# A gradient along rows of 8192 x 8192: the loads and stores of one DMA queue in groups of three instead of in strict turn

## The chip, the cores and the metric

The kernel runs on one core of a Trainium2 chip. The time is device microseconds of one execution. All differences here are a few microseconds in 1250, so fast runs are compared with fast runs of the kernel before on the same chip, and where a trace is read, it is one profiled execution. A microsecond in 1250 is 0.08%; most 95% intervals below are about 0.25% wide in all.

## The reference

```python
def reference(x: np.ndarray) -> np.ndarray:      # x: 8192 x 8192 float32
    return np.gradient(x, axis=1)
```

Inside a row the result is half the difference of the two neighbours; in the first and the last column it is the plain difference of two elements. So 268.44 MB are read and 268.44 MB are written, with almost no arithmetic.

## The kernel before

The rows are cut into 32 tiles of 128 partitions x 2 rows (8.389 MB). There are three slots in SBUF. A tile is loaded into a slot, the vector engine writes the halved differences back into the same slot, 64 elements lower, two small instructions put the end columns in place, and the slot is stored. All loads and stores are issued by the sync engine, on one queue.

```python
    def load(i):
        b = slots[i % NB]                                   # NB = 3
        ins = nc.sync.dma_start(out=b[:, SH : SH + W], in_=x_sets[i])
        loads.append(chain(i, ins, *([stores[i - NB]] if i >= NB else [])))

    with tc.manual_schedule():
        for i in range(NB):
            load(i)
        for i in range(nsets):                              # nsets = 32
            ...                                             # GpSimd: end columns; vector engine: the tile
            for r in range(0, R, nr):                       # one pass; two halves for the last tile
                ...
                ins = nc.sync.dma_start(
                    out=out_sets[i, :, r * m : (r + nr) * m], in_=b[:, r * m : (r + nr) * m]
                )
                stores[i] = chain(i, ins, placed)
                if 2 <= i and not last:
                    tc.add_manual_dep(ins.ins, stores[i - 1].ins.name, landed, reason="behind a load that has begun")
                at = [halved]
            if 1 <= i and i - 1 + NB < nsets:
                load(i - 1 + NB)
```

`chain(i, ins, needed...)` makes an instruction wait for the named ones only. The order of the queue is L0 L1 L2 S0 S1 L3 S2 L4 S3 L5 ..., with each store from S2 on (those of the last tile excepted) held back until the store before it has landed.

## Time and profile before

| | kernel before |
|---|---|
| time, median of 3 (and of 6, with the later ones) | 1250.21 us (1250.34) |
| span of the profiled run | 1247.7 us |
| vector engine busy | 554.8 us, 44% |
| DMA queue busy | 99.6% |

The lines that show the bound are in the prediction. The rows behind its last reading, that early turns are slower than late ones, are these: issue rows of the sync engine in the timeline (start, duration, engine, line, operation; the load rows between them are left out). A store is issued there at the moment the previous one has landed, so the steps between rows are the time of one load and one store.

```profile
140.42 0.34 SPq L95 DMA_DIRECT2D out_dram<-slot  x1
...
179.55 0.33 SPq L95 DMA_DIRECT2D out_dram<-slot  x1
...
218.83 0.33 SPq L95 DMA_DIRECT2D out_dram<-slot  x1
...
258.45 0.33 SPq L95 DMA_DIRECT2D out_dram<-slot  x1
...
1072.97 0.33 SPq L95 DMA_DIRECT2D out_dram<-slot  x1
...
1111.62 0.33 SPq L95 DMA_DIRECT2D out_dram<-slot  x1
...
1150.25 0.33 SPq L95 DMA_DIRECT2D out_dram<-slot  x1
```

The late steps are 38.65 and 38.63 us, the early ones half a microsecond to a microsecond longer. The DMA engines are busy in both, and the question of this study is what in the early ones is slow.

### The profile page before, as it was taken

How to read it: one execution, taken by the hardware profiler on the slowest of the kernel's cores; microseconds unless marked ns; L12 is line 12 of the kernel's file. 1: busy time of each engine (PE TensorE's matmuls, PEld its weight loads, DVE VectorE, ACT ScalarE, POOL GpSimd, SP SyncE). 2: the span in 40 equal slices, each digit the busy share in tenths (PEclk: the TensorE clock that was granted, in tenths of full speed). 3: DMA queues.
4: the chain of work that ended last, by engine and by line, in shares of the span. 5: the costliest groups of instructions: out<-in, count | busy, mean ns of one | idle time of the engine just before them, and what ended most of it. 6: DMA issues, size and time to landing. Idle time of an engine off the chain costs nothing.

```text
span 1247.7 us, 241 instructions
## 1 busy us (share of the span) xinstructions
DVE 554.8 (44%) x54; POOL 8.8 (1%) x48
## 2 busy tenths in 40 slices
DVE  2851455324553345533455334554335543355433
POOL 0000000000000000000000000000000000000000
DMA  9999999999999999999999999999999999999998
GB/s 403 437 437 424 424 429 435 435 435 431 431 437 433 427 431 433 429 435 437 437 437 435 427 431 437 427 433 437 437 437 437 435 431 429 435 433 437 431 433 357
DMA packets 9361, 536.88 MB, mean 430 GB/s; under 512 B 1040, under 2 KB 1040, under 8 KB 1040
## 3 DMA queue, kind: packets, MB, share of 16 engines
q1 hardware_dynamic: 9360, 536.88, 99.6%
q14 instruction: 1, 0.01, 0.0%
HBM read 268.44 MB, written 268.44 MB: 430 GB/s over the span
## 4 chain that ended last, share of the span: by engine, by line
another core or an unknown queue 68%; DVE 18%; DMA 8%; issue 3%; POOL 1%; POOLq 0%
DVE slot L82 18%; DMA slot<-in_x_dram 5%; DMA out_dram<-slot 3%; POOL ends L71 0%; POOL slot L93 0%; DVE slot L93 0%; POOLq L129 0%
## 5 line engine op out<-in xcount | busy, mean ns | idle before, releaser
L82 DVE CUSTOM_DVE_ANT_0 slot<-slot 128x16382 f32<-128x16382 f32 (+1 forms) x33 | 551.3, 16706 | 670.6 <-POOL ends L71 670.6
L71 POOL TENSOR_TENSOR ends<-slot 128x4 f32<-128x4 f32 x32 | 6.3, 198 | 991.5 <-DMA slot<-in_x_dram 991.5
L93 DVE COPY slot<-ends 128x4 f32<-128x4 f32 (+1 forms) x21 | 3.6, 171 | 0.7
L93 POOL COPY slot<-ends 128x4 f32<-128x4 f32 x12 | 2.3, 190 | 207.8 <-DVE slot L82 207.8
L118 POOL MEMSET const-bfloat16-1.0<- 128x1 bf16 x1 | 0.1, 102 | 0.0
L118 POOL MEMSET const-uint8-127<- 128x1 uint8 x1 | 0.1, 102 | 0.0
L118 POOL MEMSET const-float32-0.0<- 128x1 f32 x1 | 0.1, 98 | 0.2 <-issue 0.2
L118 POOL MEMSET const-float32-1.0<- 128x1 f32 x1 | 0.1, 98 | 0.0
## 6 DMA issues: line engine op xcount, KB each, us to landing
out_dram<-slot SPq DMA_DIRECT2D x2, 4096.0 KB, 20.2
slot<-in_x_dram SPq DMA_DIRECT2D x32, 57.6
out_dram<-slot SPq DMA_DIRECT2D x31, 38.6
```

The lines of the kernel that those rows point to most:

```text
L71: ins = nc.gpsimd.tensor_sub(out=ends[:, i, :, :], in0=xin[:, :, 1 : m : m - 2], in1=xin[:, :, 0 : m - 1 : m - 2],)
L82: ins = nc.vector._custom_dve(dve_ops.TENSOR_TENSOR_REDUCE_SUB_MAX, out=b[:, c0:c1], in0=b[:, SH + c0 + 1 : SH + c1 + 1], in1=b[:, SH + c0 ...
L93: ins = placer.tensor_copy(out=res[:, :, 0 : m : m - 1], in_=ends[:, i, r : r + nr, :])
L118: nc = _bacc.Bacc("TRN2", target_bir_lowering=False, num_devices=1)
```

## The change

The intent is to let the queue hold runs of three loads and three stores, and to drop the waits that kept loads and stores in strict turn. The instructions, their bytes and the slots stay as they were.

```diff
-    landed = mybir.DependencyInfo(mybir.DependencyClass.Sync, mybir.DependencyReason.DATA)
@@
                 stores[i] = chain(i, ins, placed)
-                if 2 <= i and not last:
-                    tc.add_manual_dep(ins.ins, stores[i - 1].ins.name, landed, reason="behind a load that has begun")
                 at = [halved]
-            if 1 <= i and i - 1 + NB < nsets:
-                load(i - 1 + NB)
+            if i % NB == NB - 1:
+                for k in range(i + 1, min(i + 1 + NB, nsets)):
+                    load(k)
```

The order of the queue becomes L0 L1 L2 S0 S1 S2 L3 L4 L5 S3 S4 S5 ..., and ends L30 L31 S30 and the two halves of S31. The places where a store follows a load fall from 30 to 11, those where a load follows a store from 29 to 10.

> **What bounds the kernel now.** I read the page's shares of busy time first, then the slices, then the issue rows of the sync engine in the timeline, then its waits, then stretches of the span beside each other.
>
> ```profile
> span 1247.7 us, 241 instructions
> DVE 554.8 (44%) x54; POOL 8.8 (1%) x48
> ...
> DMA  9999999999999999999999999999999999999998
> GB/s 403 437 437 424 424 429 435 435 435 431 431 437 433 427 431 433 429 435 437 437 437 435 427 431 437 427 433 437 437 437 437 435 431 429 435 433 437 431 433 357
> ...
> q1 hardware_dynamic: 9360, 536.88, 99.6%
> ```
>
> The vector engine works 44% of the span and GpSimd 1%; the one DMA queue keeps 16 engines busy for 99.6% of it. No slice shows a hole. So the kernel is bound by moving 536.88 MB, and the order of the queue can only matter if it changes the rate or opens holes.
>
> The steady state, in the timeline of one full turn (a column of start, one of duration):
>
> ```profile
> 724.99 0.33 SPq L95 DMA_DIRECT2D out_dram<-slot  x1
> 725.36 0.43 SPq L61 DMA_DIRECT2D slot<-in_x_dram  x1
> 744.29 0.20 POOL L71 TENSOR_TENSOR ends<-slot 128x4 f32<-128x4 f32 x1 [20.92 <-DMA slot<-in_x_dram]
> 744.52 17.22 DVE L82 CUSTOM_DVE_ANT_0 slot<-slot 128x16382 f32<-128x16382 f32 x1 [21.40 <-POOL ends L71]
> 761.78 0.17 DVE L93 COPY slot<-ends 128x4 f32<-128x4 f32 x1
> 763.62 0.33 SPq L95 DMA_DIRECT2D out_dram<-slot  x1
> 764.00 0.43 SPq L61 DMA_DIRECT2D slot<-in_x_dram  x1
> 782.95 0.20 POOL L71 TENSOR_TENSOR ends<-slot 128x4 f32<-128x4 f32 x1 [38.46 <-DMA slot<-in_x_dram]
> ```
>
> Each store is issued at the instant the previous store has landed, and GpSimd starts the instant a load has landed. So a store landed at 724.99, a load at 744.29, a store at 763.62, a load at 782.95: steps of 19.30, 19.33 and 19.33 us, with no difference between the two directions and nothing added at a switch. A tile is 128 partitions x 16384 x 4 bytes = 8.389 MB; 8.389 / 19.32 = 434.2 GB/s. From a load's landing to a finished tile is 761.78 + 0.17 - 744.29 = 17.66 us, less than one transfer.
>
> The waits of the sync engine, total, count, longest:
>
> ```profile
> SPq L95 <- DMA out_dram<-slot: 1082.2, 29, 38.8
> SPq L61 <- DMA out_dram<-slot: 21.5, 1, 21.5
> ```
>
> These 1082.2 us look like a cost and are none: the sequencer waits for the previous store while the load queued behind that store is still to come, which is 19.3 us of work for the DMA engines. The chain of waits on the page puts 68% under "another core or an unknown queue" and 18% under the vector engine; with the DMA slices at 9 throughout, I don't take that attribution as a bound.
>
> Last, the start of the span and later stretches (width, vector busy, GpSimd busy, clock, DMA share, GB/s):
>
> ```profile
> 3.00:60.00 57.00, 34.62 (x3) 0.59 (x3) 1.00 0.99 423
> 105.00:395.00 290.00, 121.25 (x11) 1.98 (x11) 1.00 1.00 432
> 700.00:1185.00 485.00, 223.05 (x20) 3.52 (x18) 1.00 1.00 434
> ```
>
> The DMA is busy in all of them, yet the early rate is a little lower than the late one. The first issue rows show the same: store issues at 140.42, 179.55, 218.83, 258.45 and 297.75 are 39.13, 39.28, 39.62 and 39.30 us apart, where late ones are 38.63. This is all the waste there is. If the first load lands at 22.56 (the issue at 0.74 plus 21.82 in the chain in order of time) and the other 63 transfers took 19.32 us each, the last would land at 22.56 + 63 x 19.32 = 1239.7 us. The span is 1247.7, of which about 1 us is the end after the last landing. So some 7 us, 0.6%, are lost to slow packets, nearly all in the first half.
>
> **What the Trainium skill says.** (1) DMA: Bandwidth & Descriptors, section "Where 436 GB/s comes from": the 16 ports give 435.2 GB/s in all. The trace agrees: 434.2 GB/s in the steady turn is 99.8% of that, for loads and for stores. (2) The same page, section "Anatomy of one DMA": DMA engines don't wait on semaphores, the issuing sequencer does. So an order can only open a hole if the sync engine issues too late; the trace has issues 19 us ahead of need. (3) The same page, section "Queues, rings and completion order": on each engine the descriptors are consumed in ring order. That fits the landings above, which come in the order of issue, and lets me lay out the new order as a simple row of transfers. I found no section that gives a cost for switching between loads and stores; here the trace decides, and it shows none in steady state.
>
> **The change part by part.** Removed: 29 waits of a store for the landing of the previous store. They delayed only the sequencer; worth 0 us by themselves. Added: nothing; the same 32 loads and 33 stores, with the same bytes and same descriptors. The work of the vector engine and GpSimd is the same: 33 x 16.706 us = 551.3 us in all, still hidden if the DMA doesn't wait for it. Moved: the loads of tiles 3k+3 to 3k+5 now stand behind the stores of 3k to 3k+2. Switches of direction fall from about 62 to about 21, worth 0 us each by the steady steps.
>
> Now the new row, with 19.32 us a transfer from the landing of load 2 at about 62 us (GpSimd's start on tile 2 in the trace is at 62.22). Stores 0, 1, 2 are ready at 40.3, 59.7 and 79.9, and are due at 62, 81 and 101: at least 21 us early. Load 3 is issued when store 0 has landed and store 2 was issued, at 81.5; it is due at 120. Load 4 at 101, due at 139; load 5 at 120, when load 3 begins, due at 159. So each load is issued about two transfers (38.6 us) ahead. Load 3 lands at 139, so store 3 is ready at 139 + 17.7 = 157 and due when load 5 ends at 178: 21 us early (2 x 19.32 - 17.66 = 21.0). Store 4 is ready at 158.5 + 17.7 = 176 and due at 197; store 5 at 195.5, due at 217. Load 6 must follow store 5 in program order (195.5) and store 3's landing (197): issued at 197, due at 236. That closes a cycle of 6 x 19.32 = 115.9 us for three tiles, with a smallest slack of 21.0 us, against 115.9 us for three turns of before. No hole opens.
>
> The tail: 32 = 10 x 3 + 2, so the last group has two loads, then store 30, then the two halves of store 31. Store 30 is ready 17.7 us after its load, while load 31 takes 19.32: 1.7 us early. That is the smallest slack of all, and it occurs once. The first half of tile 31 needs 0.2 + 8.7 + 0.2 us, the second as much again, both inside store 30's 19.32. So the row again ends with the same three stores, back to back, as before. Sum: 0 us from waits, 0 from switches, 0 from holes. The 7 us of early slow packets stay to be settled.
>
> **The rivals.**
> Rival A, the early loss belongs to switches: fewer of them would take away up to two thirds of 7 us, giving about 1245.5 us. For it: the early turns of 39.1 to 39.6 us all contain switches. Against it: the late turns contain as many and cost nothing; and three loads in a row, 3 to 60 us, have only 423 GB/s.
> Rival B, the early loss belongs to loads (engines that read in step, or something that passes with time) and comes with grouped loads as well, or a little more because three follow each other: 1250 to 1256 us. For it: the rate of the first three loads, which know no switch; GpSimd's starts on tiles 3 to 6 at 120.92, 160.17, 199.47 and 239.14 with the store issues between show loads of 19.6 to 20.3 us and stores of about 19.4. This is my main case, at the same loss.
> Rival C, the queue runs dry: if a store had to wait for its tile, each group would lose a part of one transfer, 11 x 19.3 = 212 us at most, so some 1460 us. The slack of 21 us per store speaks against it, and the vector engine at 44% too.
> Rival D, the deeper queue: up to four transfers are outstanding now, against three before. A sequencer that blocks on a full ring would delay an issue that has 20 to 38 us of slack. No cost expected.
> Rival E, long runs of stores are slower than single ones. The trace has two in a row, stores 0 and 1, landing at about 81.5 and 101.3 (the load issue and the next store issue at those times): 19.4 and 19.8 us. If each of 32 stores took 0.4 us more, that would be 13 us, 1263 us: still within 2%.
>
> **Range and chances.** The median is 1250.2 us before; my sum moves it by 0, with A pulling to 1245 and B to 1256. I predict 1250 us, 8 in 10 between 1244 and 1257. Faster by over 2% means below 1225, under the 1239.7 that the DMA rate alone allows: chance 0.01. Slower by over 2% means above 1275, and needs C or a slowdown I can't see: 0.03. The rest, 0.96, is within 2%.
>
> **What would show each step right or wrong.** The DMA line should stand at 9 in all slices, the queue's share at 99 to 100%. The sync engine's rows should show three stores about 19 us apart, then loads issued as each store lands, a cycle of 115.9 us late in the span, and its long waits moved from stores waiting for stores to loads waiting for stores and stores for the vector engine or GpSimd. Vector busy time should stay near 555 us. Late steps other than 19.32 us within a run of loads or stores would refute the claim that switches are free; a hole in the DMA slices once per group would make C right; an early loss clearly under 7 us would make A right, one over it B in its stronger form. I would be wrong by more than the range if a run of three loads or stores had another rate than a single one.

## The result, and the profile after

The changed kernel took 1247.49 us (median of 6 runs, 1246.68 to 1248.03) against 1250.34 us before (6 runs, 1249.39 to 1251.82). A ratio here is the mean time of one kernel's fast runs over that of the other's of the same rounds, so it is not quite the ratio of these medians: 0.9976, with a 95% interval of 0.9963 to 0.9989. The change is worth some 3 us or a quarter of a per cent, by the verdict at 2% "same", and the interval leaves out 1.

The page of the changed kernel, busy times, DMA slices and queue:

```profile
span 1245.0 us, 241 instructions
DVE 554.8 (45%) x54; POOL 8.8 (1%) x48
...
DMA  9999999999999999999999999999999999999999
...
q1 hardware_dynamic: 9360, 536.88, 99.8%
```

Compute is unchanged, and the DMA is busy throughout, as before. The sync engine's own waits (for whom, us in total, times, longest):

```profile
SPq L94 <- DVE slot L92: 525.7, 21, 55.9
SPq L60 <- DMA out_dram<-slot: 373.2, 29, 19.2
SPq L94 <- POOL slot L92: 298.8, 12, 36.7
```

The 1082.2 us of stores waiting for stores are gone, and 1197.7 us of other waits stand in their place. None of them is time that the kernel loses: the sequencer has nothing to do in either version. This is how to read a wait on a sequencer that only issues transfers: its length says little, only whether it ended in time does. The issue rows of the changed kernel show that:

```profile
157.57 38.99 SPq L94 DMA_DIRECT2D out_dram<-slot  x3
197.84 39.18 SPq L60 DMA_DIRECT2D slot<-in_x_dram  x3
273.61 39.05 SPq L94 DMA_DIRECT2D out_dram<-slot  x3
313.93 39.12 SPq L60 DMA_DIRECT2D slot<-in_x_dram  x3
...
1203.88 19.93 SPq L94 DMA_DIRECT2D out_dram<-slot  x3
1205.53 0.20 POOL L70 TENSOR_TENSOR ends<-slot 128x4 f32<-128x4 f32 x1 [19.14 <-DMA slot<-in_x_dram]
```

A row with "x3" is three issues, and its duration runs from the first to the last. Store 3 is issued at 157.57 and is due when load 5 lands, at about 178.5; load 6 at 197.84, two transfers before it is due. The smallest margin is at the end: store 30 is issued at 1203.88 and load 31 has landed on all engines at 1205.5 (the last line).

So where do the 2.7 us of the span come from? For that I used two records of the trace that have no view: the time at which each of the 16 DMA engines finished its share of each transfer, and the duration of each 64 KB packet (2.418 us when nothing disturbs it). "Landing" below is the last of the 16, "spread" the last less the first. "Loss" is what the last landing is later than the first landing plus 63 transfers of 19.32 us.

| trace | first landing | last landing | loss, us | spread at the end of the loads, us | packets more than 0.1 us slow | their excess, us over all engines | of it where a store follows a load |
|---|---|---|---|---|---|---|---|
| before | 22.56 | 1246.82 | 7.1 | 5.6 | 160 | 58.8 | 56.2 |
| after | 22.63 | 1244.12 | 4.3 | 2.6 | 95 | 38.8 | 37.0 |

(Packets of the first 6 us are left out, since every kernel has the same slow ones there.) In both kernels some 95% of the excess is of packets under way while a load with a store behind it was landing (from half a microsecond before its first engine finished to half a microsecond after its last). Those stretches are 13% of the span in the kernel before and 2% in the changed one. In the trace before, the spread grows from 0.6 us to 5.4 us in the first 630 us, and after that the steps are 19.32 us with hardly a slow packet; in the changed kernel it grows to 2.6 us. So the picture is: at such a place some engines lose part of a microsecond, those that lose fall behind, and once the engines are far enough apart the losses stop. (The packet records don't name their engine, so that it is the same engines that lose and fall behind is inferred.) How long the loads with a store behind them took in the changed kernel, from landing to landing (the third load of each of the first nine groups; 19.35 us is the undisturbed figure):

```text
load 2: 20.41 us   load 5: 19.36   load 8: 19.36   load 11: 19.39
load 14: 19.85     load 17: 19.95  load 20: 20.01  load 23: 19.52  load 26: 19.62
```

### The profile page after: what moved, and what is told of

It is laid out like the page before. It is cut to its first block, busy times and chain, and to the rows that moved or that the text cites. A ratio compares the mean times of both kernels' runs of the same rounds, so it can differ in the third digit from the quotient of the medians.

```text
span 1245.0 us, 241 instructions
## 1 busy us (share of the span) xinstructions
DVE 554.8 (45%) x54; POOL 8.8 (1%) x48
## 4 chain that ended last, share of the span: by engine, by line
another core or an unknown queue 74%; DVE 18%; DMA 3%; issue 2%; POOL 1%; SPq 0%; POOLq 0%
DVE slot L81 18%; DMA slot<-in_x_dram 3%; POOL ends L70 0%; POOL slot L92 0%; SPq L60 0%; DVE slot L92 0%; POOLq L127 0%
```

## The experiments

Theory S (switch): time is lost where a store follows a load, so fewer such places lose less. Rival L (load): each load loses a little, whatever follows it. Rival W (wait): the removed waits, or the deeper queue without them, are the gain. The results of all runs in one table; "places" are those where a store follows a load.

| kernel | places | time, us | before of the same call, us | ratio (95%) | loss in its trace, us | spread, us |
|---|---|---|---|---|---|---|
| e1_no_wait: strict turn without the waits | 30 | 1250.13 | 1250.64 | 0.9996 (0.9984 to 1.0009) | 6.3 | 5.2 |
| e2_pairs: groups of two | 16 | 1249.32 | 1250.64 | 0.9992 (0.9980 to 1.0005) | 6.2 | 5.2 |
| e4_after_again: the change | 11 | 1247.57 | 1250.64 | 0.9977 (0.9964 to 0.9989) | 4.9 | 2.7 |
| e9_far_stores: the change, other addresses | 11 | 1247.98 | 1250.48 | 0.9981 (0.9968 to 0.9995) | 6.4 | 4.0 |
| e12_eights: groups of eight | 4 | 1244.63 | 1249.77 | 0.9953 (0.9940 to 0.9965) | 2.1 | 1.2 |
| e3_one_switch: all loads, then all stores | 1 | 1243.72 | 1250.64 | 0.9945 (0.9932 to 0.9959) | 1.1 | 0.7 |
| e10_near_switch: the same, other addresses | 1 | 1244.23, one run | 1250.48 | state unknown | 1.8 | 0.4 |
| e11_early_switch: three loads, all stores, 29 loads | 1 | 1245.88 | 1249.77 | 0.9964 (0.9950 to 0.9977) | 2.9 | 1.0 |
| e5_half_turn: half tiles, strict turn | 59 | 1251.72 | 1249.62 | 1.0010 (0.9987 to 1.0034) | other sizes | 6.1 |
| e6_half_sixes: half tiles, groups of six | 11 | 1250.94 | 1249.62 | 1.0005 (0.9981 to 1.0028) | other sizes | 4.2 |
| e7_two_queues | mixed | 1254.15, fast runs alone | 1249.62 | 1.0015 (0.9963 to 1.0067) | | up to 15 |
| e8_staggered: before, engines set apart first | 30 | 1255.57 | 1249.62 | 1.0041 (1.0012 to 1.0070) | 0.4 | 6.5 |

The loss is of one profiled execution, the time of several. Kernels marked wrong below give wrong values on purpose; they move the same number of bytes.

**e1_no_wait**: the kernel before, without its waits of stores for stores.

```diff
-                if 2 <= i and not last:
-                    tc.add_manual_dep(ins.ins, stores[i - 1].ins.name, landed, ...)
```

> The kernel before without its 29 waits of a store for the previous store's landing; strict turn stays, 30 places where a store follows a load. Switch theory (time is lost where a store follows a load): as before, 1250.3 us plus or minus 1, with slow packets again at the ends of loads in the first half. Wait theory (the removed waits are what gained 2.9 us): 1247.5, as the changed kernel.

Measured: 1250.13 us, ratio 0.9996. Its sequencer waits:

```profile
SPq L95 <- DVE slot L93: 701.7, 20, 38.2
SPq L95 <- POOL slot L93: 425.4, 12, 37.3
SPq L61 <- DMA out_dram<-slot: 72.3, 29, 21.6
```

The waits moved as much as they did in the changed kernel, and the time did not move. In the same call every run of it (1248.86 us and more) was slower than every run of the changed kernel (e4_after_again, 1248.60 us and less). Rival W is out: the gain is from the order. The slow packets (161) are again at the places where a store follows a load: 53.1 of 53.8 us of excess.

**e2_pairs**: groups of two.

```diff
-            if i % NB == NB - 1:
-                for k in range(i + 1, min(i + 1 + NB, nsets)):
+            if i % 2 == 1:
+                for k in range(i + 2, min(i + 4, nsets)):
                     load(k)
```

> Groups of two loads and two stores in the same three slots: 16 places where a store follows a load, against 30 in strict turn and 11 in groups of three; 32 loads in all three. Switch theory: between the two, 1247.8 to 1249.5 us, and slow packets only at the ends of the second load of each pair. Load theory (each load loses a little, whatever follows it) has no reason for a difference to strict turn: 1250.

Measured: 1249.32 us, within what theory S expected, but the interval includes 1, so as a time it tells nothing apart. The trace does, in part: 40.8 of 42.0 us of excess lie at the 16 places, and 101 of the 105 slow packets. The loss (6.2 us) is that of strict turn without waits (6.3), and the spread ends where that one's does (5.2). So half the places did not halve the loss: it comes more slowly, but by the end of the kernel 16 places have brought the engines as far apart as 30 did.

**e3_one_switch**, wrong on purpose: 32 loads with all their vector work, then 32 stores.

```diff
+        for i in range(nsets):
+            ...                                   # the same work on tile i
+            if i + NB < nsets:
+                load_next(i + NB)                 # waits for the work on tile i, not for a store
+        for i in range(nsets):
+            j = nsets - NB + i % NB               # the last three tiles, over and over
+            ...                                   # store slot j % NB to out_sets[i]
```

> Wrong result on purpose: all 32 loads, with the same vector work on each tile, then all 32 stores (of the last three tiles, over and over). The same bytes, one place where a store follows a load. Switch theory: the loss of 7 us of before shrinks to that of one switch, about 1 us: span 1241 to 1242.5, time 1243 to 1245 us. Load theory: the loss stays with the loads, 1247 us or more. If runs of one direction were themselves slower or faster, the late steps would leave 19.32 us.

Measured: 1243.72 us, ratio 0.9945: 6.9 us under the kernel before, as theory S expected, and a rival L that puts the loss on loads is out, for here are the same 32 loads. How it looks at the third load, in the timeline (GpSimd starts when a load has landed), first in the changed kernel, then in this one:

```profile
42.04 0.20 POOL L70 TENSOR_TENSOR ends<-slot 128x4 f32<-128x4 f32 x1 [19.14 <-DMA slot<-in_x_dram]
...
62.45 0.20 POOL L70 TENSOR_TENSOR ends<-slot 128x4 f32<-128x4 f32 x1 [2.71 <-DMA slot<-in_x_dram]
```

```profile
42.03 0.20 POOL L76 TENSOR_TENSOR ends<-slot 128x4 f32<-128x4 f32 x1 [19.15 <-DMA slot<-in_x_dram]
...
61.38 0.20 POOL L76 TENSOR_TENSOR ends<-slot 128x4 f32<-128x4 f32 x1 [1.64 <-DMA slot<-in_x_dram]
...
80.73 0.20 POOL L76 TENSOR_TENSOR ends<-slot 128x4 f32<-128x4 f32 x1 [19.15 <-DMA slot<-in_x_dram]
...
100.09 0.20 POOL L76 TENSOR_TENSOR ends<-slot 128x4 f32<-128x4 f32 x1 [1.65 <-DMA slot<-in_x_dram]
```

Load 2 takes 20.41 us with store 0 behind it, and 19.35 with load 3 behind it. Two details missed my expectation. The one switch that is left cost nothing (load 31 took 19.35 us, the first store 19.33). And runs of one direction are not quite at 19.32: loads took 19.35, stores 19.29 to 19.33 (but for one of 19.54, in the middle of the run); the 31 steps of 19.35 make up 0.9 of the 1.1 us of loss. One packet in the whole trace was more than 0.1 us slow, apart from the start; it lies in that one store.

**e4_after_again**: the changed kernel, beside the three above.

> The changed kernel once more, beside the others on this chip: 1247.5 us plus or minus 0.7, ratio to before 0.9976. A second trace of it tells which of its slow switches come back: the one after load 2 (1.0 us) should, the later ones of 0.2 to 0.7 us (in groups 8 to 16 of the first trace) may not.

Measured: 1247.57 us, ratio 0.9977, so the result repeats. Load 2 took 20.48 us, as before. Loads 5, 8 and 11 took 19.39, 19.50 and 19.34, load 14 took 20.16 (19.85 in the first trace), load 17 19.57 (19.95), load 20 19.71 (20.01), load 29 20.10 (19.35). In both traces the first place costs over 1 us, and the later ones from 0 to 0.8 us, another amount in each.

**e5_half_turn and e6_half_sixes**: half tiles, in strict turn (59 places) and in groups of six (11 places).

```diff
-    R = 2
-    NB = 3
+    R = 1
+    NB = 6
```

e5 is e1_no_wait with this edit, e6 is the changed kernel with it.

> Strict turn with tiles of half the size (6 slots, 64 tiles, no waits between stores): 59 places where a store follows a load. Half-size transfers took 9.68 us in the tail of the kernel before, 0.04 us per pair over a full one, so 64 x 0.04 = 2.5 us more whatever the order. Linear switch theory (each such place costs the slowest engine some 0.3 us, without end): 1250.3 + 2.5 + 29 x 0.3 = 1261 us. Saturating switch theory (the losses push the 16 engines apart, and stop when they are about 5 us apart, as they do in the traces of strict turn and of pairs): 1252 to 1254 us, spread of the last landings 5 to 6 us.

> The changed order with tiles of half the size: six loads, then six stores, 11 places where a store follows a load, as in the changed kernel. Both switch theories: the changed kernel's 1247.5 plus 2.5 us for the halves, 1249 to 1251 us, spread 2 to 3 us. If the number of transfers rather than of switches mattered, it would be as slow as the strict turn of halves.

Measured: 1251.72 and 1250.94 us. The linear form of theory S (1261 us) is out: 59 places cost no more than the first 18 or so, and the spread stopped at 6.1 us after about 400 us, from where on the steps hold at 9.64 to 9.73. But e6 is a half miss. Its time is in the range, yet its spread is 4.2 us and not 2 to 3, and it is only 0.8 us faster than e5, where the two intervals overlap almost wholly. The count of places alone doesn't set the loss. Full tiles scatter as well: at the same 11 places the spread ended at 2.6, 2.7 and, in e9_far_stores, 4.0 us. And the trace of e6 shows where most of the gain went. The median step was 9.71 us for a load and 9.68 for a store, while the late turns of e5, past their losses, average 9.68 over both. By an estimate from these medians, 127 steps of 0.017 us cost e6 about 2.2 us in its runs, while what is lost beyond them fell from 6.1 to 3.1 us. Why a load inside a run of loads is a little slower (here as in e3_one_switch) I can't say.

**e7_two_queues**: strict turn without waits, with the stores on the scalar engine's queue.

```diff
-                ins = nc.sync.dma_start(
+                ins = nc.scalar.dma_start(
                     out=out_sets[i, :, r * m : (r + nr) * m], in_=b[:, r * m : (r + nr) * m]
```

> The loads on the sync engine's queue and the stores on the scalar engine's queue, each issued as soon as its slot or tile is ready; correct result. Loads and stores can then be in progress at the same time on every engine all along. If a switch from a load to a store costs each engine 0.3 us by itself, packets of 2.4 us that alternate would lose over 10%: above 1370 us. If the cost arises only where all 16 engines change together, about the time of before, 1243 to 1260 us.

Measured: four runs of 1254.15, 1247.53, 1257.29 and 1267.61 us, the last of state slow; the verdict on the fast three is "same", with an interval of 1% in all. The page shows both queues moving half each:

```profile
q1 hardware_dynamic: 4608, 268.44, 49.7%
q10 hardware_dynamic: 4752, 268.44, 49.5%
```

A cost per packet is out (that would have been above 1370 us). What the two queues show in the trace is a wider spread: landings of one transfer lay up to 15 us apart. The time of the fast runs differs by 10 us, but so did that of the kernel before in the same call (1247.90 to 1258.82 us, all of state fast), so the scatter can't be put down to the queues. The Trainium skill, DMA: Bandwidth & Descriptors, section "Issuing engines are not separate DMA queues", says that a second issuing engine saves only sequencer time; in this case's runs it saved nothing that can be told from the noise.

**e8_staggered**: the kernel before, with four small extra loads in front.

```diff
+        extra = {1: [], 2: []}
+        for n, p in enumerate((8, 4, 2, 1)):
+            k, at = 1 + n // 2, SH + (n % 2) * m
+            ins = nc.sync.dma_start(out=slots[k][0:p, at : at + m], in_=x_sets[0, 0:p, 0:m])
+            extra[k].append(chain(k, ins))
         for i in range(NB):
-            load(i)
+            ...                                   # load i, behind the extra loads of its slot
```

> The kernel before with four small extra loads first, on 8, 4, 2 and 1 partitions, a packet of 32 KB each, so that the engines start their real work 0, 1.2, 2.4, 3.6 or 4.8 us late and stay apart. Saturating switch theory (a switch costs only while the engines are in step): the landing steps are 19.32 us from early on, the spread stays at 5 to 6 us, and the time is that of before within 2 us (the 4.9 us of extra loads take the place of the later loss). Theory that the loss of a switch does not depend on the spread: extra loads plus the old loss, 1250.3 + 4.9 = 1255 us, spread 8 to 10 us.

Measured: 1255.57 us, which is the number of the wrong theory, and still the trace speaks for the saturating one. Two lines of the stretches view (stretch, width, vector and GpSimd busy, clock, DMA share, GB/s) and four issue rows of stores:

```profile
0.70:10.00 9.30, 0.00 (x0) 0.00 (x0) 1.00 0.98 137
...
40.00:700.00 660.00, 307.23 (x29) 4.74 (x24) 1.00 1.00 434
```

```profile
112.29 0.33 SPq L103 DMA_DIRECT2D out_dram<-slot  x1
...
150.91 0.33 SPq L103 DMA_DIRECT2D out_dram<-slot  x1
...
189.53 0.33 SPq L103 DMA_DIRECT2D out_dram<-slot  x1
...
228.19 0.33 SPq L103 DMA_DIRECT2D out_dram<-slot  x1
```

The steps are 38.62, 38.62 and 38.66 us from the start, where the kernel before has 39.13 to 39.62 in the same stretch. The spread is 6.1 us at the first landing and 6.5 at the end. From the first landing (35.00 us) to the last (1252.52) the kernel loses 0.4 us at 30 places, against 7.1. After those loads, over all engines, 32 packets were slow, with 9.0 us of excess, against 160 and 58.8, so the other engines lost little too. What I mis-sized is the cost of the extra loads: they ran at 137 GB/s beside the first real load, which landed at 35.00 us instead of 22.56, so 12.4 us late and not 4.9. 12.4 - 7.1 + 0.4 = 5.7 us, and 5.95 were measured between the medians.

**e9_far_stores and e10_near_switch**, both wrong on purpose: does the address matter? The first sends the stores of the changed kernel 16 tiles away, the second starts the stores of e3_one_switch at tile 29.

```diff
-                    out=out_sets[i, :, r * m : (r + nr) * m], ...
+                    out=out_sets[(i + 16) % nsets, :, r * m : (r + nr) * m], ...            # e9
+                    out=out_sets[(i + nsets - NB) % nsets, :, r * m : (r + nr) * m], ...    # e10
```

> Wrong result on purpose: the changed kernel with each store of tile i sent to the place of tile i + 16 (modulo 32) in the output; order, waits and bytes are the same, 11 places where a store follows a load. In every trace so far the first such place (load 2, store 0) cost about 1.0 us, while the only one of the single-switch kernel (load 31, store 0) cost nothing although its engines were as much in step. Address theory (what a switch costs depends on how the stored addresses lie to those still being read; here they are 14 tiles apart instead of 2): the 1.0 us after load 2 goes, and the time falls below 1246.7 us, towards 1243.7. Position theory (it is the early place that costs, whatever the address): 1247.5 us, 1.0 us after load 2 again.

> Wrong result on purpose: the single-switch kernel with its stores starting at the place of tile 29 instead of 0, so that the one store behind a load (load 31, then the store to 29) lies two tiles below it, as load 2 and store 0 do in the changed kernel. Address theory: load 31 now takes about 1.0 us longer than 19.35. Position theory: 19.35 us again, no slow packet.

Measured: 1247.98 us for the first, ratio 0.9981, and load 2 took 20.16 us again; for the second, load 31 took 19.35 us. As far as these two go, the distance of the stored addresses from those being read doesn't set the cost of a place. (The expectation's "every trace so far" passes over e8_staggered, where load 2 took 19.33 us, and the half tiles, where the first place cost 0.6 us.) The trace of e10 also shows a loss without a switch: between 46 and 81 us, with nothing but loads in progress, 35 packets were slightly slow (5.5 us over all engines), and loads 2 to 4 took 19.57, 19.77 and 19.42 us. So a place where a store follows a load isn't the only thing that can cost time. (The profiled run of e9 was the slowest of its five, 1249.35 us, so its loss of 6.4 us stands a little high.)

**e11_early_switch**, wrong on purpose: L0 L1 L2, all stores, 29 loads.

```diff
+        for i in range(NB):
+            compute(i)
+            store(i, i)                           # tile i to out_sets[i]
+        for i in range(NB, nsets):
+            store(i, i % NB)
+        ...                                       # then loads 3 to 31, with the work on each
```

> Wrong result on purpose: loads of tiles 0 to 2, then all 32 stores (of these three tiles over and over), then the other 29 loads. One place where a store follows a load, as in the single-switch kernel, but the early one, load 2 and store 0; and one change from stores to loads, late. Position theory (the early place costs 1.0 us whatever follows): load 2 takes 20.3 us, everything after it 19.30 to 19.36, the last landing about 1.0 us later than with the late single switch, so some 1241.9 us into the span. If the change from stores to loads costs as well, load 3 takes over 19.4 us. The time of this one is not comparable to 0.5 us, since its end is a load.

Measured: load 2 took 20.07 us, 0.7 over 19.35, so the early place costs about what it does elsewhere even with 32 stores behind it. But the rest was not flat: the last store took 19.93 and load 3 took 19.95 us, 1.2 us lost where a load follows a store. In the traces of before and after the same kind of place has at most 1.1 of 58.8 us of excess. So my theory, in which only the other direction costs, is too narrow: here the first change of direction after a long run of stores cost as much.

**e12_eights**, wrong on purpose: groups of eight loads and eight stores.

```diff
+        for g in range(0, nsets, 8):
+            ...                                   # 8 loads, the work on each
+            for q in range(8):
+                store(g + q, g + 5 + q % NB)      # the last three tiles of the group
```

> Wrong result on purpose: groups of eight loads and eight stores (of the last three tiles of the group), four places where a store follows a load, all of them behind a run of eight loads. Switch theory, with what the groups of three and the single switch gave: between 1243.7 and 1247.5 us, at 1244.5 to 1246 us, slow packets only at the ends of loads 7, 15, 23 and 31. If a switch behind a long run costs nothing, as load 31 did, 1243.7 us and no slow packets.

Measured: 1244.63 us, in the expected range. Load 7, the first with a store behind it, took 20.00 us, the other three such loads 19.35 to 19.36. 25 of the 29 slow packets lie at these four places. But of the 2.1 us of loss a second 0.6 is of load 27, which took 19.95 us in the middle of a run of loads; the expectation has no place for that.

## Why the prediction was right or wrong

**The bound, the waits, the row of transfers: right.** The time was 1247.5 us, in the range of 1244 to 1257 and within 2%. That alone says little for the mechanism: the range was wide enough for A and for B, and the value it named, 1250 us with no gain, was missed: the interval of the ratio (0.9963 to 0.9989) does not include 1. The waits are worth nothing: e1_no_wait, 0.9996. No hole opened: the DMA line stands at 9 in every slice, and the issue times I laid out are those of the trace (store 3 at 157 foretold and 157.57 measured, load 6 at 197 and 197.84, store 30 1.7 us early and 1.6). One refinement: 1.6 us is the margin against the slowest engine. With a spread of 2.6 us the fastest engine had finished load 31 a microsecond before store 30 was issued, and waited. The end was not delayed, since the slowest engine sets it (the last full transfer took 19.35 us), but the margin was in truth already negative for the fastest.

**"Switches of direction ... worth 0 us each by the steady steps": wrong.** This is the step that failed. The steady steps were read from the second half of the trace, where the engines were already 5 us apart, and applied to the first half, where they were not. With the same bytes, 30, 16, 11, 4 and 1 places where a store follows a load took 1250.1, 1249.3, 1247.6, 1244.6 and 1243.7 us, and 94 to 99% of the slow packets' excess lies at these places in the traces with 30, 16, 11 and 4 of them. My count of 62 changes of direction before was also a little high; it is 59.

**The rivals.** I took B, the loads, as the main case, and it was wrong: e3_one_switch keeps the 32 loads and loses the loss. The evidence I had for B was misread. The 423 GB/s of the stretch from 3 to 60 us come back in e3_one_switch, where no store is near and nothing is lost there (423 again), so they were no sign of a slow load; nor do the first three loads "know no switch", for load 2 has store 0 behind it and took 20.25 us. And that loads took 19.6 to 20.3 us and stores 19.4 was a sign of what stands behind each load. B's other form, something that passes with time, doesn't fit either: e8_staggered has steady steps from the start, and e4_after_again still lost 0.75 us at load 29, over 1100 us into the span. A was the right one, and its estimate of two thirds of 7 us, 4.7 us, was too high: 2.9 us between the medians. It was too high because the loss isn't in proportion to the number of places but tends to a limit near a spread of 5 to 6 us (16 places reach 5.2, 59 places 6.1), while 11 places had got to 2.6 to 4.0 when the kernel ended. C, D and E did not occur: no hole, no gain or loss from the depth of the queue, and stores inside a run took 19.29 to 19.40 us each (the last of an early run 19.57, with the load behind it 0.2 us shorter than the others).

**The cycle: nearly right.** Foretold were 115.9 us late in the span; the first stores of the groups are issued 116.04 us apart early (157.57 to 273.61) and 116.28 late (971.64 to 1087.92).

**What stays open.** Why a change of direction costs anything on engines in step, and hardly anything on engines 5 to 6 us apart, is not shown; e8_staggered shows only that it is so. Why the first such place costs 0.6 to 1.1 us in every kernel of one queue where it comes early and the engines are in step, the next ones often nothing, and later ones up to 0.95 (load 6 of the kernel before), and why the single late one of e3_one_switch and e10_near_switch is free, is open too; the addresses tried did not explain it. So are the losses away from any place in e10_near_switch and e12_eights, and those of e11_early_switch where a load follows a store. No correct version tried here beats the changed kernel: a run of loads can be no longer than the buffer that takes it, and the three slots are already full when the stores begin. Larger groups were only to be had with wrong results.

## What to carry to other kernels

When one queue is saturated, look for what is left not in the waits but in how steady the transfers are, and read "costs nothing" from the stretch that the change will affect, not from the calmest one. Where buffers allow, longer runs of loads and of stores are slightly better than strict turn (here 0.25% with runs of three, some 0.5% with one run of each, that one with wrong results), and the issue times needed for it come for free as long as each transfer is issued well ahead. A wait on a sequencer that only issues transfers can be a thousand microseconds long and worth nothing.

## What the Trainium skill lacked or had wrong

- DMA: Bandwidth & Descriptors has nothing on changes between loads and stores in one queue. The runs show up to 1.1 us at such a place, and 1250.1 us with 30 places against 1243.7 us with one for the same bytes.
- The same page doesn't say that the 16 engines of one queue drift apart and stay so: the shares of one transfer finished within 0.6 us of each other at the start and 5.6 us apart at the end of the loads of the kernel before.
- The same page's section "Issuing engines are not separate DMA queues" says what a second issuing engine saves, not that the shares of one transfer may then finish further apart: up to 15 us in the trace of e7_two_queues, against 5.7 us at most in the kernel before, with one queue.
- HBM Reference, section "Specifications (TRN2)", gives about 425 GB/s for a core streaming alone. The steady turn here moved 434 GB/s, loads and stores taken together, and the run of loads in e3_one_switch 433.5 GB/s (8.389 MB in 19.35 us).
